# A hybrid decoder trunk in split float32: sums of squares added up before the matmuls that take them, and four transfers moved in their queue

## The chip, the cores and the metric

The kernel runs on one core of one Trainium2 chip. The metric is the device time of one execution in microseconds (us), as the median of repeated executions. A core has TensorE (PE, with the weight loads as PEld), VectorE (DVE), ScalarE (ACT), GpSimd (POOL) and SyncE (SP), which issues nearly all DMAs of this kernel.

## The reference

Two layers act on 528 tokens (16 learned meta tokens, then 512 of the sequence) of width 1024. Per layer, cut to what matters here:

```python
h = rmsnorm(x)
u, z, c_q, c_kv, k_rope, z_mla, g_pool, g_mla = split(h @ W_in)   # 512 512 768 256 32 512 1024 1024
y_pool = W_pool_up(pool_mix(u) * silu(z))
q = rmsnorm(c_q) @ w_q_b          # 8 heads of 64 plain + 32 rotary columns
k, v = rmsnorm(c_kv) @ w_kv_b     # 8 heads of 64 + 64; k_rope joins every head's k
q, k = rope(rmsnorm(q)), rope(rmsnorm(k))          # over the 96 columns of a head
y_mla = W_mla_up(causal_softmax(q k / sqrt(96)) v * silu(z_mla))
x = x + W_out(sigmoid(g_pool) * y_pool + sigmoid(g_mla) * y_mla)
```

Every `rmsnorm` needs a sum of squares over a row: over the 1024 columns of `x`, over the 256 columns of `c_kv`, and over the 96 columns of each head's `q` and `k`. The output is the last `x` without the meta tokens.

## The kernel before, in words

**Layout.** Activations lie with features on the 128 partitions and tokens along the free axis; the 528 tokens are two halves of 264 (`FULL`). Sums over features are thus sums over partitions, and the kernel takes them with matmuls against a matrix of ones or of 0/1 columns.

**GEMMs.** Each float32 operand is split in a high and a low float32r part. `wload` brings a weight chunk of 128 x 512 by a DMA on SP into `raw` (3 buffers), ACT copies it to the high part `whi` (L200), DVE subtracts for the low part `wlo` (L201). `mm3` then issues three matmuls per product: L205 (high x high), L206 (high weights x low data), L207 (low weights x high data). `stream` walks the list `plan` of all GEMMs chunk by chunk; the other work is placed between its steps by `step()`, by `fill_now(ns)`, which advances the stream by a modelled time on TensorE, by `gap()` (four in every head, of about `FILL` ns), and by `after(ns, fn)`, which runs `fn` when the modelled clock has gone on by `ns`. `behind(a, b)` makes `a` wait for `b`; `follow(a, b)` only keeps the order. Within these bounds the framework's scheduler orders each engine's queue, and every engine works through its queue in order.

**Sums of a layer's start.** In layer 0 `row_sums` loads the tokens once more in rows (`xrow`, eight tiles of 128 x 512, and `mrow`, the meta tokens, 32 x 512), and ACT squares each with a running sum into `sx` (L400). Two writes bring `sx` to the DRAM tensor `nsr` (L404 the 512 tokens, L405 the 16 meta tokens). In layer 1 ACT squares the eight tiles of `x` in `square_x` (L378) and POOL adds them in two groups of four (L382). `norm_sums` then sums the squares `csq` of the two tiles of `c_kv` (ACT, L485), and in layer 1 the two groups of `xsq`, with matmuls of 32 ones columns (L426). Four of these fill the four column groups of the array side by side. `kr_sums` (L501) follows on PE. The sums go to `nsr`, come back as `nq` (L448) with the tokens spread over 16 partitions, `newton` on DVE makes inverse roots, and `ndr` (L458) and two broadcast reads (L465) bring them to `rinv` and `q1`. DVE's rows of `tables`, and then the sine and cosine on ACT (L332, L333), stand behind it.

**Sums of the heads.** `ev_qr` and `ev_qn` empty the accumulators of the queries, and `q_stat` squares them on ACT (L730); keys are squared likewise (L677). `stat_go` (L535) sums all squares with float32 matmuls of 128 x 16 by 264 columns, each `behind` the last square of the batch, in four column groups side by side; a query's 32 rotary rows and 64 plain rows come in different matmuls with different columns of the constant `cst` (`C_IR` and `C_IK`). `qk_stats` puts `fill_now(LAG + 100)` ahead of it.

**Heads.** `head` computes scores (L881 and L205 to L207 into `S`), exponentials (L840), and DVE turns the blocks of probabilities (L846, `attD`). SP writes them to `pdr` (L906), writes the inverse row sums to `rdr` (L907), and `back` later reads the blocks in another order in four DMAs (L915, `attE`) and the row sums as a broadcast (L920). `parts` splits `attE` in two parts (ACT L958, DVE L959) and `pv` (L980, L983 into `o`) multiplies by the values. For odd heads `gate` multiplies by the row sums on POOL, and `meta_turn` sends a block of the meta tokens through `mdr` (L945, L941). The value weights `wvb` are loaded whole into `attD` (two DMAs of 256 KB; a GEMM with a `home`).

Of the kernel before, what the change touches and what calls it, by code (L numbers as in the profile page):

```python
# [9 lines left out]
F32 = mybir.dt.float32  # L10
# [4 lines left out]
ALU = mybir.AluOpType  # L15
# [16 lines left out]
TWO_PI = 2.0 * math.pi  # L32
SWAP = [i ^ 16 for i in range(32)]
# [19 lines left out]
FILL = (2620.0, 2530.0)  # L53
# [27 lines left out]
def trunk(ctx, tc, xT, xrow, mrow, pos, win, wkr, wqb, wkb, wvb, wgr, wpu, wmu, wout, gains, const, yT):  # L81
# [108 lines left out]
    loads = [0]  # L190
# [147 lines left out]
    nsr = [dp.tile([4, T], F32, name=f"nsr{l}") for l in range(DEPTH)]  # L338
# [9 lines left out]
    class Layer:  # L348
        def __init__(self, l):
# [11 lines left out]
            self.sq, self.half = [], halves()  # L361
# [14 lines left out]
        def square_x(self, k):  # L376
            self.xsq[k] = slot(f"cq{4 + k}" if k < 4 else f"q{k}")
            made = act.activation(self.xsq[k][:, :T], self.xt[k][:, :T], AF.Square)  # L378
            for w in (1, 2):
# [4 lines left out]
        def row_sums(self):  # L384
            sx = sm.tile([P, 2, 5], F32, tag="sx", name=nm("sx"))
            tags = ("q4", "q5", "q6", "q7", "kn0", "kn1", "kn2", "bc", "bc")
            rows = []
            for i in range(2 * len(tags) + 4):
# [3 lines left out]
                if i % 2 == 0 and len(rows) < len(tags):  # L392
                    k = len(rows)
                    r, src = (P, xrow[:, k]) if k < 8 else (2 * NM, mrow)
                    rows.append(slot(tags[k], bufs=3 if tags[k] == "bc" else 1)[0:r, 0:512])
                    behind(sp.dma_start(rows[k], src), newest[0])
                if i % 2 == 1 and i >= 5:
                    k = (i - 5) // 2
                    t = rows[k]
                    made = act.activation(t, t, AF.Square, accum_out=sx[0:t.shape[0], k % 2, k // 2:k // 2 + 1])  # L400
# [4 lines left out]
            sp.dma_start(raw[0:2, 0:NM].rearrange("h m -> m h"), sx[0:2 * NM, 0, 4:5])  # L405

        def norm_sums(self):
# [10 lines left out]
            px, pc = mmt() if self.l else None, mmt()  # L418
            xs = self.xsq[::4] if self.l else []
            runs = [(px, t, m, m < 2, m >= len(xs) - 2) for m, t in enumerate(xs)]  # L420
            runs += [(pc, t, m, True, True) for m, t in enumerate(self.csq)]
            for k in range(0, len(runs), 2):
                for s, (a, b) in enumerate(FULL):
                    for ps, t, m, start, stop in runs[k:k + 2]:
                        g = 64 * s + 32 * (m % 2)
                        mm = pe.matmul(ps[g:g + 32, :HALF], ones[:, 0:32], t[:, a:b], start=start, stop=stop,  # L426
                                       tile_position=(0, g))
                        if t is not self.csq[1]:
                            behind(mm, self.csq_last)
            self.kr_sums()  # L430
            sums = tmp()
            for s, (a, b) in enumerate(FULL):
                if self.l:
                    act.activation(sums[0:64, a:b], px[64 * s:64 * s + 64, :HALF], AF.Copy)
                dve.tensor_copy(sums[64:128, a:b], pc[64 * s:64 * s + 64, :HALF])
            raw, norms = nsr[self.l], ndr[self.l]
            if self.l:
                sp.dma_start(raw, sums[0:97:32, 0:T])
            else:
                sp.dma_start(raw[2:4], sums[64:97:32, 0:T])  # L440
                for _ in rows:
# [4 lines left out]
            nq = sm.tile([16, 4, C], F32, tag="nq", name=nm("nq"))  # L446
# [3 lines left out]
            dve.scalar_tensor_tensor(out=na[:, 0, :], in0=nq[:, 1, :], scalar=1.0 / D, in1=na[:, 0, :],  # L450
                                     op0=ALU.mult, op1=ALU.add)
            dve.tensor_scalar(na[:, 1, :], na[:, 0, :], EPS, None, op0=ALU.mult)
            dve.tensor_scalar(ny[:, 2, :], na[:, 1, :], EPS, None, op0=ALU.mult)
            for m in range(2):
                dve.scalar_tensor_tensor(out=na[:, 1, :], in0=nq[:, 2 + m, :], scalar=1.0 / 256,
                                         in1=na[:, 1, :], op0=ALU.mult, op1=ALU.add)
# [268 lines left out]
        def q_stat(self, ps, a, b, c):  # L725
            for a0, b0 in FULL:
                a0, b0 = max(a, a0), min(b, b0)
                if a0 < b0:
                    q = next(self.half)
# [566 lines left out]
```

## Time and profile before

| | |
|---|---|
| Median of 3 runs | 756.11 us (755.23 to 756.22) |
| Profiled execution | 756.64 us, of which the traced span is 754.9 us |
| Granted TensorE clock in it | 1.000 |
| PE busy | 749.7 us (99% of the span) |
| PEld / DVE / ACT / POOL busy | 682.9 / 548.1 / 395.9 / 218.8 us |
| DMA | 106.58 MB, mean 141 GB/s |

A row of the timeline gives start and duration in us, then engine, line, operation, output and input tiles, shapes and count, and in brackets the idle time ahead of it and what ended that. A row of the groups gives the busy time in us and the mean of one in ns. A row of the waits gives who waited for whom, the total in us, how often, and the longest. `SPq` is SyncE's queue. A float32 matmul (L426, L501, L535) leaves two records in the trace, one per pass, so a count there is twice the number of matmuls. Records of pipelined matmuls overlap: what one costs is the distance to the start of the next.

### The profile page before, as it was taken

The numbers are of one execution on the slowest core, as the hardware profiler recorded it, in microseconds if no ns is written. First come the engines' busy times: TensorE is split into PE (matmuls) and PEld (weight loads), VectorE is DVE, ScalarE is ACT, GpSimd is POOL, SyncE is SP. The second block draws the span as 40 slices with busy tenths as digits, with TensorE's granted clock in tenths as the row PEclk, the third lists the DMA queues.
The fourth block names the chain that finished last, engine by engine and source line by source line (L and its number), as shares of the span: only waits on it lengthen the run. The fifth ranks groups of instructions, "written<-read, shape, count | busy, mean of one in ns | idle before, by whom it ended". The sixth has DMA issues, their size and how long they took to land.

```text
span 754.9 us, 14329 instructions
## 1 busy us (share of the span) xinstructions
PE 749.7 (99%) x5038; PEld 682.9 (90%) x5038; DVE 548.1 (73%) x1209; ACT 395.9 (52%) x866; POOL 218.8 (29%) x267
## 2 busy tenths in 40 slices
PE   9999999999999999999999999999999999999998
PEld 8999899999999999999997898887788888888887
DVE  5588777457999988684466477676478999975942
ACT  6755655645565665542355446456345666653321
POOL 1126404204463620061130264023044435111400
PEclk9999999999999999999999999999999999999999
DMA  8532223443765567525642322234447756773472
GB/s 316 162 108 89 74 82 86 113 116 119 211 186 166 151 194 192 156 86 157 183 145 85 114 84 66 89 90 120 108 135 210 190 156 181 195 200 93 127 227 84
DMA packets 72853, 106.58 MB, mean 141 GB/s; under 512 B 14102, under 2 KB 34966, under 8 KB 72780
## 3 DMA queue, kind: packets, MB, share of 16 engines
q1 hardware_dynamic: 72636, 105.39, 47.6%
q8 instruction: 40, 0.66, 0.4%
q14 instruction: 33, 0.27, 0.1%
q10 hardware_dynamic: 144, 0.26, 0.1%
HBM read 89.76 MB, written 15.86 MB: 140 GB/s over the span
## 4 chain that ended last, share of the span: by engine, by line
PE 98%; DMA 1%; ACT 0%; SPq 0%; issue 0%; DVE 0%; ACTq 0%
PE mm L205 29%; PE mm L207 29%; PE mm L206 29%; PE S L205 2%; PE S L207 2%; PE S L206 2%; PE o L980 1%; PE o L983 1%; PE S L535 1%; PE S L881 1%; DMA attE<-pdr 1%; PE S L501 0%; DMA xb<-xT 0%; PE mm L995 0%; PE mm L426 0%
## 5 line engine op out<-in xcount | busy, mean ns | idle before, releaser
L205 PE MATMUL mm<-hh,whi 128*128 128x264 f32 (+2 forms) x1072 | 336.1, 315 | 0.6 <-ACT whi L200 0.6
L206 PE MATMUL mm<-hl,whi 128*128 128x264 f32 (+2 forms) x1072 | 336.6, 315 | 0.0
L207 PE MATMUL mm<-hh,wlo 128*128 128x264 f32 (+2 forms) x1072 | 336.4, 316 | 0.0
L201 DVE TENSOR_TENSOR wlo<-raw,whi 128x512 fp32r<-128x512 f32 (+2 forms) x238 | 173.4, 730 | 95.8 <-ACT whi L200 92.4
L200 ACT ACTIVATE whi<-raw 128x512 fp32r<-128x512 f32 (+2 forms) x238 | 142.3, 600 | 176.1 <-PE mm L206 136.4
L205 PEld LDWEIGHTS mm<-hh,whi 128*128 128x128 f32 x1072 | 201.3, 188 | 15.0 <-issue 0.8
L206 PEld LDWEIGHTS mm<-hl,whi 128*128 128x128 f32 x1072 | 201.6, 188 | 12.9
L207 PEld LDWEIGHTS mm<-hh,wlo 128*128 128x128 f32 x1072 | 200.9, 188 | 12.3
L649 POOL TENSOR_TENSOR racc<-racc,tmp 128x264 f32<-128x264 f32 (+1 forms) x15 | 14.4, 959 | 132.3 <-ACT tmp L648 132.3
L1055 POOL TENSOR_TENSOR tmp<-tmp,xb 128x264 f32<-128x264 f32 (+1 forms) x24 | 27.0, 1137 | 49.1 <-DVE tmp L1053 46.4
L833 DVE CUSTOM_DVE_ANT_0 S<-S,maskw,nqs 128x240 f32<-128x240 f32 (+4 forms) x80 | 37.8, 492 | 4.2 <-PE S L207 3.9
L811 POOL CAST qhl<-q 32x528 fp32r<-32x528 f32 (+1 forms) x32 | 25.1, 800 | 44.2 <-PE S L881 42.9
L809 POOL CAST kh<-cq 32x528 fp32r<-32x528 f32 x16 | 15.6, 976 | 69.8 <-issue 36.1
L206 PE MATMUL mm<-th,whi 128*128 128x264 f32 (+1 forms) x108 | 34.7, 321 | 0.0
L205 PE MATMUL mm<-cq,whi 128*128 128x264 f32 (+1 forms) x108 | 34.7, 321 | 0.0
L205 PE MATMUL mm<-u,whi 128*128 128x264 f32 (+1 forms) x108 | 34.6, 321 | 0.0
L206 PE MATMUL mm<-cq,whi 128*128 128x264 f32 (+1 forms) x108 | 34.5, 321 | 0.0
L207 PE MATMUL mm<-cq,wlo 128*128 128x264 f32 (+1 forms) x108 | 34.5, 321 | 0.0
L207 PE MATMUL mm<-u,wlo 128*128 128x264 f32 (+1 forms) x108 | 34.5, 319 | 0.0
L959 DVE TENSOR_TENSOR attE<-attE,th 128x640 fp32r<-128x640 f32 x32 | 26.9, 862 | 3.7 <-ACT th L958 3.7
L840 ACT ACTIVATE cq<-S,bia 128x400 f32<-128x400 f32 (+2 forms) x48 | 24.4, 511 | 9.2 <-DVE bia L894 7.7
L843 POOL COPY pm<-cq 128x16 f32<-128x16 f32 x32 | 18.2, 570 | 37.7 <-ACT cq L840 37.5
(301 smaller groups left out, 1369.5 us busy)
## 6 DMA issues: line engine op xcount, KB each, us to landing
raw<-win SPq DMA_DIRECT2D x143, 256.0 KB, 3.2
pdr<-attD SPq DMA_DIRECT2D x16, 640.0 KB, 3.7
attE<-pdr SPq DMA_DIRECT2D x64, 160.0 KB, 3.9
raw<-wout SPq DMA_DIRECT2D x32, 256.0 KB, 2.8
raw<-wpu SPq DMA_DIRECT2D x16, 256.0 KB, 2.7
raw<-wmu SPq DMA_DIRECT2D x16, 256.0 KB, 2.7
raw<-wqb SPq DMA_DIRECT2D x12, 256.0 KB, 2.6
xb<-xT SPq DMA_DIRECT2D x8, 264.0 KB, 5.5
```

What stands on the lines that cost most here:

```text
L200: act.activation(hi[:, :n], raw[:, :n], AF.Copy)
L201: dve.tensor_sub(lo[:, :n], raw[:, :n], hi[:, :n].bitcast(F32))
L205: first = pe.matmul(out, wh, xh, start=start, stop=False)
L206: pe.matmul(out, wh, xl, start=False, stop=False)
L207: newest[0] = pe.matmul(out, wl, xh, start=False, stop=stop)
L809: gp.tensor_copy(d[r0:r0 + 32, :], f[g0:g0 + 32, :])
L811: gp.tensor_copy(d[r0:r0 + 32, x0:T], f[g0:g0 + 32, x0:T])
L833: return dve.tensor_tensor_reduce(out=sv, in0=sv, in1=mask, scale=nqs[:, i, h:h + 1], scalar=3e38, op0=ALU.add, op1=ALU.min, accum_out=bia ...
L840: act.activation(pv, sv, AF.Exp, scale=-1.0, bias=bia[:, i:i + 1], accum_out=rs[:, c:c + 1])
L843: gp.tensor_copy(pm[:, i, 16 * odd:16 * odd + 16], pt[i][:, 0:NM])
L959: dve.tensor_sub(got[:, a:b], f[:, a:b], hi[:, a:b].bitcast(F32))
L1055: gp.tensor_add(t[:, :b - a], t[:, :b - a], self.am[m][:, a:b])
```

## The change

1. **Fewer matmuls for sums.** POOL adds the squares of the second `c_kv` tile to those of the first ahead of the matmuls (new line, L425 after), and in layer 1 the two groups of `xsq` are added as well (one more addition at what is now L388). `norm_sums` then has 2 matmuls in layer 0 instead of 4, and 4 in layer 1 instead of 8. In `q_stat` the squares of a query's rotary rows are added to the squares of its plain rows (L740 after), 32 partitions at a time, on POOL for the pairs of heads 0 to 2 and on DVE for pair 3; `stat_go` then has 20 matmuls per layer instead of 24. The rotary columns change seats inside a group of four heads (`SEAT`) so that the partitions match.
2. **Smaller tensors of sums.** `nsr` has 3 rows in layer 0 and 2 in layer 1 instead of 4; one or two small DVE operations and, in layer 1, ACT's two copies of the sums (L434) go.
3. **Meta tokens first.** `row_sums` loads and squares the meta tokens first; their write to `nsr` leaves at once, and the write of the 512 tokens is the last.
4. **Value weights later.** The two DMAs of `wvb` wait for a matmul four weight loads back.
5. **Row sums behind the blocks.** The write of `rdr` comes after the four reads of `attE`, its read a third of `BACK` later, and the last head's `gate` after `BACK` instead of `LATE`.
6. **Numbers.** `LAG + 100` becomes `LAG + 700`, `FILL` goes from (2620, 2530) to (2583, 2493), and `mu1` of layer 0 uses the ordinary weight buffers.

```diff
     def wload(src, n, spare, home=None):
-        raw = early.pop(0) if early else fetch(src, n, rawt() if home is None else home, sp)
+        if home is not None:
+            raw = home
+            behind(sp.dma_start(raw, src), marks[-4])
+        else:
+            raw = early.pop(0) if early else fetch(src, n, rawt(), sp)
         loads[0] += 1
+        marks.append(newest[0])
...
-                    r, src = (P, xrow[:, k]) if k < 8 else (2 * NM, mrow)
+                    r, src = (P, xrow[:, k - 1]) if k else (2 * NM, mrow)
...
+                    if k == 0:
+                        meta = sp.dma_start(raw[0:2, 0:NM].rearrange("h m -> m h"), sx[0:2 * NM, 0, 4:5])
                 yield
-            raw = nsr[0]
-            sp.dma_start(raw[0:2, NM:T].rearrange("h (p i) -> p h i", i=4), sx[:, :, 0:4])
-            sp.dma_start(raw[0:2, 0:NM].rearrange("h m -> m h"), sx[0:2 * NM, 0, 4:5])
+            follow(sp.dma_start(raw[0:2, NM:T].rearrange("h (p i) -> p h i", i=4), sx[:, :, 0:4]), meta)
...
+            ps, c = mmt(), self.csq[0]
+            self.csq_last = gp.tensor_add(c[:, :T], c[:, :T], self.csq[1][:, :T])
+            runs = [(self.xsq[0], 0)] * self.l + [(c, 32)]
+            for i, (a, b) in enumerate(FULL):
+                for t, m in runs:
+                    g = 64 * i + m
+                    mm = pe.matmul(ps[g:g + 32, :HALF], ones[:, 0:32], t[:, a:b], start=True, stop=True,
+                                   tile_position=(0, g))
+                    behind(mm, self.csq_last)
...
+                    eng = dve if p == 3 else gp
+                    for g in (0, 64):
+                        g += 32 * (p % 2)
+                        made = eng.tensor_add(q[g:g + 32, :n], q[g:g + 32, :n], self.rsq[p // 2, a0][g:g + 32, :n])
+                    self.stat(q[:, :n], a0, b0, C_IK + 6 - 2 * p, made)
...
-            sp.dma_start(row.rearrange("a (p i) -> p (a i)", i=4), rs[:, 0:4])
...
+                    read = sp.dma_start(got[0][32 * b:32 * b + 32, :].bitcast(F32).rearrange("k (a x) -> k a x", a=4),
+                                        via[:, n * b:n * b + n].rearrange("(a k) x -> k a x", a=4))
+                    behind(read, newest[0])
+                follow(sp.dma_start(row.rearrange("a (p i) -> p (a i)", i=4), rs[:, 0:4]), read)
+                after(BACK / 3, sums)
```

**In SP's queue, layer 0, at the sums.** `xrow` and `mrow` are the tokens in rows, `sx` their sums, `nsr` the tensor of sums, `nq` its read, `raw` the weight chunks. Before:

```order
L396 DMA kn_57_393<-xrow 128x512
L396 DMA bc_414<-xrow 128x512
L396 DMA bc_440<-mrow 32x512
L135 DMA raw_601<-win 128x512
L440 DMA nsr_117<-tmp_474 2x528
L135 DMA raw_643<-win 128x512
L404 DMA nsr_117<-sx_257 128x2x4
L135 DMA raw_689<-win 128x512
L405 DMA nsr_117<-sx_257 16x2x1
L448 DMA nq_563<-nsr_117 16x4x33
```

After:

```order
L136 DMA raw_498<-win 128x512
L409 DMA nsr_117<-sx_257 16x2x1
L402 DMA kn_53_373<-xrow 128x512
L136 DMA raw_542<-win 128x512
L402 DMA kn_57_394<-xrow 128x512
L402 DMA bc_415<-xrow 128x512
L136 DMA raw_599<-win 128x512
L402 DMA bc_441<-xrow 128x512
L136 DMA raw_641<-win 128x512
L442 DMA nsr_117<-tmp_474 1x528
L411 DMA nsr_117<-sx_257 128x2x4
L136 DMA raw_687<-win 128x512
```

The meta tokens' write (16x2x1) moves from last to nine rows ahead of the tokens' write (128x2x4), which is now the last one that the read of `nq` (next row) needs.

**In POOL's queue, layer 1, ahead of the sums of the heads.** L575/L576 (L578/L579 after) are the rotation of queries, L811 (L821) copies for the first heads, `attD` and `attE` hold the squares here. Before:

```order
L576 TENSOR_TENSOR q_1186_6872<-q_1186_6872,tmp_6876 128x512
L575 TENSOR_TENSOR q_1197_6916<-q_1197_6916,tcos 128x512
L811 COPY qhl_107<-q_1184_6870 32x512
L811 COPY qhl_109<-q_1184_6870 32x512
L576 TENSOR_TENSOR q_1197_6916<-q_1197_6916,tmp_6920 128x512
L811 COPY qhl_108<-q_1185_6871 32x512
L811 COPY qhl_110<-q_1185_6871 32x512
L809 COPY kh_7319<-cq_1276_7313 32x528
```

After:

```order
L821 COPY qhl_107<-q_1184_6874 32x512
L821 COPY qhl_109<-q_1184_6874 32x512
L579 TENSOR_TENSOR q_1197_6920<-q_1197_6920,tmp_6924 128x512
L821 COPY qhl_108<-q_1185_6875 32x512
L821 COPY qhl_110<-q_1185_6875 32x512
L740 TENSOR_TENSOR attD_6964<-attD_6964,xb 32x248 x2
L740 TENSOR_TENSOR attD_6964<-attD_6964,xb 32x264 x2
L740 TENSOR_TENSOR attD_6964<-attD_6964,xb 32x248 x2
L740 TENSOR_TENSOR attD_6964<-attD_6964,xb 32x264 x2
L740 TENSOR_TENSOR attE_7043<-attE_7043,xb 32x248 x2
L740 TENSOR_TENSOR attE_7043<-attE_7043,xb 32x264 x2
L819 COPY kh_7348<-cq_1280_7342 32x528
```

Twelve additions stand behind the last of those copies, and the matmuls of L535 (L538 after) read what they write. On PE the same order lists 1111 matmuls of the GEMMs ahead of layer 0's `stat_go` before and 1120 after, 3651 and 3656 ahead of layer 1's, and 153 and 168 ahead of layer 0's L426 (L430 after).

**In SP's queue, layer 1, the last two heads.** Before:

```order
L906 DMA pdr_125<-attD_8383 128x1280
L135 DMA raw_8755<-win 128x512
L907 DMA rdr_142<-rs_8381 128x4
L915 DMA attE_8600<-pdr_125 32x4x320 x4
L920 DMA cq_1544_8605<-rdr_142 64x512
L135 DMA raw_8781<-win 128x512
L906 DMA pdr_126<-attD_8545 128x1280
L907 DMA rdr_143<-rs_8544 128x4
L135 DMA raw_8805<-win 128x512
L945 DMA mdr<-cq_1549_8640 128x256
L915 DMA attE_8701<-pdr_126 32x4x320 x4
L920 DMA cq_1544_8605<-rdr_143 64x512
```

After:

```order
L916 DMA pdr_125<-attD_8398 128x1280
L136 DMA raw_8772<-win 128x512
L924 DMA attE_8615<-pdr_125 32x4x320 x4
L927 DMA rdr_142<-rs_8396 128x4
L934 DMA cq_1558_8707<-rdr_142 64x512
L136 DMA raw_8798<-win 128x512
L916 DMA pdr_126<-attD_8560 128x1280
L136 DMA raw_8821<-win 128x512
L959 DMA mdr<-cq_1548_8653 128x256
L924 DMA attE_8716<-pdr_126 32x4x320 x4
L927 DMA rdr_143<-rs_8559 128x4
L136 DMA raw_8853<-win 128x512
```

The write of the row sums (`rdr`), which waits for DVE, no longer stands between the write of the blocks and their reads.

More of the change, by code (lines that the diff above doesn't have):

```diff
@@ L51 @@
 N_GAIN = 24
-FILL = (2620.0, 2530.0)
+FILL = (2583.0, 2493.0)
 RESERVE = ("gm3", "gm3")
@@ L337, in trunk @@
     scr = dp.tile([P, 8, SEQ], F32, name="scr")
-    nsr = [dp.tile([4, T], F32, name=f"nsr{l}") for l in range(DEPTH)]
+    nsr = [dp.tile([3 - l, T], F32, name=f"nsr{l}") for l in range(DEPTH)]
     ndr = [dp.tile([3, T], F32, name=f"ndr{l}") for l in range(DEPTH)]
@@ L378, in square_x @@
             made = act.activation(self.xsq[k][:, :T], self.xt[k][:, :T], AF.Square)
-            for w in (1, 2):
+            for w in (1, 2, 4):
                 if k % (2 * w) == 2 * w - 1:
@@ L386, in row_sums @@
             tags = ("q4", "q5", "q6", "q7", "kn0", "kn1", "kn2", "bc", "bc")
-            rows = []
+            rows, raw = [], nsr[0]
             for i in range(2 * len(tags) + 4):
@@ L417, in norm_sums @@
                     next(rows)
[L418 to L429, printed above, removed]
+            ps, c = mmt(), self.csq[0]
[7 more added lines that the diff above has]
+                    behind(mm, self.csq_last)
             self.kr_sums()
@@ L728, in q_stat @@
                 if a0 < b0:
[L729 to L731 removed]
+                    q, n = next(self.half), b0 - a0
+                    made = act.activation(q[:, :n], ps[:, a0 - a:b0 - a], AF.Square)
+                    if r is not None:
+                        self.rsq[r, a0] = q
+                        continue
+                    eng = dve if p == 3 else gp
[3 more added lines that the diff above has]
+                    self.stat(q[:, :n], a0, b0, C_IK + 6 - 2 * p, made)
         def ev_qr(self, r):
@@ L927, in head @@
             if odd == 1:
-                after(LATE, gate)
+                after(LATE if h + 1 < H else BACK, gate)
             return h, got
@@ L1233, in constants @@
     c[64:128, C_IK + 15] = 1.0
-    for i in range(4):
-        c[32 * i:32 * i + 32, C_IR + 12 + i] = 1.0
     c[0:32, C_KPE:C_KPE + 8] = 1.0
@@ L1266, in arrange @@
     no, ro = np.arange(64), 64 + np.arange(32)
-    cols = np.concatenate([QK * h + ro for h in range(H)] + [QK * h + no for h in range(H)])
+    cols = np.concatenate([QK * (h - h % 4 + SEAT[h % 4]) + ro for h in range(H)] + [QK * h + no for h in range(H)])
     wqb = tiles(w_q_b[:, :, cols])
```

50 lines of the change are left out of this document (24 added, 26 removed).

## The prediction

> **What bounds the kernel now.** The page comes first: the span, the busy time of the engines, and the engines of the chain that ended last.
>
> ```profile
> span 754.9 us, 14329 instructions
> PE 749.7 (99%) x5038; PEld 682.9 (90%) x5038; DVE 548.1 (73%) x1209; ACT 395.9 (52%) x866; POOL 218.8 (29%) x267
> PE 98%; DMA 1%; ACT 0%; SPq 0%; issue 0%; DVE 0%; ACTq 0%
> ```
>
> TensorE works 99% of the span, and the chain lies on it for 98%. So a change gains only by what it takes out of PE's queue, or by a wait of PE's that goes; it loses by every new wait. Next the waits of PE; the view lists three, and two of them lie in the start, up to the first GEMM matmul, where nothing is changed:
>
> ```profile
> PE mm L205 <- ACT whi L200: 0.6, 1, 0.6
> ```
>
> So one wait of 0.6 us stands in the body. The profiled run took 756.64 us, span 754.9, so 1.74 lie outside the span. The median of the three runs is 756.11, 0.53 less; the sum is made against the profiled run and its difference is applied to the median.
>
> **Part 1, fewer matmuls.** From the chain in order of time, the sums of squares:
>
> ```profile
> 24.81 0.58 PE mm L426 x8
> 149.32 2.80 PE S L535 x48
> 405.28 1.03 PE mm L426 x16
> 528.08 2.80 PE S L535 x46
> ```
>
> 24 matmuls per layer at L535 leave 48 records and take 2.80 us: four column groups run side by side, so that is six sets of four at 2.80 / 6 = 0.467. The change leaves 20 matmuls, five sets: **-0.467 in each layer, -0.93**. At L426 in layer 1, eight matmuls (two sets, 1.03) become four (one set); one set is priced in layer 0, four matmuls in 0.58: **-0.45**. In layer 0 four matmuls become two. Priced by count that would save 0.29; but the two keep both passes of 264 columns, and the four ran side by side in one set's time. Between 0.29 and nothing I take **0**. Sum -1.38.
>
> What these matmuls wait for is now later. POOL's additions are priced by rows of its own; the trace has no two-input addition on 32 partitions.
>
> ```profile
> L382 POOL TENSOR_TENSOR q<-q,q 128x528 f32<-128x528 f32 x3 | 4.8, 1584 | 9.1 <-ACT q L378 9.1
> L649 POOL TENSOR_TENSOR racc<-racc,tmp 128x264 f32<-128x264 f32 x10 | 7.9, 791 | 63.8 <-ACT tmp L648 63.8
> L649 POOL TENSOR_TENSOR racc<-racc,tmp 128x512 f32<-128x512 f32 x5 | 6.5, 1295 | 68.4 <-ACT tmp L648 68.4
> L515 POOL COPY kp<-kp 32x264 f32<-32x264 f32 x12 | 6.2, 520 | 8.1 <-DVE kp L513 7.6
> L576 POOL TENSOR_TENSOR q<-q,tmp 128x264 f32<-128x264 f32 x4 | 3.6, 910 | 0.5 <-DVE tmp L574 0.4
> ```
>
> *Layer 0, start.* ACT's last `c_kv` squares, the row square behind them, and PE's L426; for layer 1, ACT's last `c_kv` square:
>
> ```profile
> 21.72 0.66 ACT L485 ACTIVATE q<-mm 128x264 f32<-128x264 f32 x2
> 22.26 0.63 ACT L400 ACTIVATE q<-q 128x512 f32<-128x512 f32 x1
> 24.74 0.65 PE L426 MATMUL mm<-q,ones 128*32 128x264 f32 x8
> ...
> 401.48 0.39 ACT L485 ACTIVATE q<-mm 128x264 f32<-128x264 f32 x1 [0.79 <-DVE kl L483]
> ```
>
> The squares end at 22.38. In the new order two row squares (0.63 each) and one `whi` (about as long) come ahead of the last of them, so it ends near 24.3; POOL's addition of 128x528 (1.58) ends near 25.9. PE's place is 15 GEMM matmuls later (168 instead of 153); one stands for 0.12 (rows of part 3), 1.8 together, thus 26.5. Some 0.6 us remain: cost 0, or up to 0.6 if ACT or POOL is later by twice that.
>
> *Layer 1, start.* The `xsq` tiles are squared long before; the `c_kv` addition follows ACT's last square, which ends at 401.9, and ends near 403.5, before L426 at 405.3. Cost 0.
>
> *The heads' sums.* ACT's last square and PE's L535 in layer 0, and POOL's last work ahead of L535 in layer 1, and DVE's price:
>
> ```profile
> 146.43 0.40 ACT L730 ACTIVATE attE<-mm 128x264 f32<-128x264 f32 x1
> 514.34 1.71 POOL L811 CAST qhl<-q 32x512 fp32r<-32x512 f32 x2
> L507 DVE TENSOR_TENSOR kp<-S,kp 32x264 f32<-32x264 f32 x12 | 5.1, 428 | 0.4
> ```
>
> Layer 0 had 149.3 - 146.8 = 2.5 us between the last square and L535, and gets nine matmuls more (1120 instead of 1111), 1.1 us. Four DVE additions at 0.43, two of them behind the last square, fit. In layer 1 POOL is free from 516.05; twelve additions have to end before L535, which stood at 528.0 and moves by five matmuls of 512 columns (about 0.23 each), to 529.2. That leaves 13.1 / 12 = **1.09 us per addition**. One takes at least 0.52 (a copy of the same shape) and at most 1.30 (128x512, twice the columns); I take 0.91, the addition of rotated queries, since operand and engine load are nearest. Twelve then end at 527.0: cost 0, with 2.5 us at the upper end.
>
> **Parts 2 and 3, the meta tokens first.** The one wait of PE's body, and the work that it hangs on:
>
> ```profile
> 56.94 0.28 PE L206 MATMUL mm<-kl,whi 128*128 128x264 f32 x1
> 57.06 0.28 PE L207 MATMUL mm<-kh,wlo 128*128 128x264 f32 x1
> 57.97 0.36 PE L205 MATMUL mm<-hh,whi 128*128 128x264 f32 x1 [0.62 <-ACT whi L200]
> ...
> 55.98 1.14 ACT L200 ACTIVATE whi<-raw 128x512 fp32r<-128x512 f32 x2
> ...
> 56.64 0.83 DVE L201 TENSOR_TENSOR wlo<-raw,whi 128x512 fp32r<-128x512 f32 x1 [1.04 <-ACT whi L200]
> 57.40 0.76 DVE L584 TENSOR_TENSOR u<-mm,rinv 128x264 f32<-128x264 f32 x2
> ```
>
> From start to start a matmul takes 0.12; here 0.91 pass, so the wait costs **0.79**. The matmul starts a new accumulator, and at 57.8 DVE frees one (L584), behind a `wlo` that waited for ACT. ACT had been held by the sine block and DVE by `newton` and the angles, which begin when `nq` lands:
>
> ```profile
> 31.80 0.66 SPq L405 DMA_DIRECT2D nsr<-sx  x1
> 36.01 0.35 SPq L448 DMA_DIRECT2D nq<-nsr  x1
> ...
> nsr<-sx SPq DMA_DIRECT2D x1, 4.0 KB, 3.1
> nsr<-sx SPq DMA_DIRECT2D x1, 0.1 KB, 4.1
> ...
> 38.62 0.17 DVE L449 TENSOR_SCALAR na<-nq 16x33 f32<-16x33 f32 x1 [4.70 <-DMA nq<-nsr]
> ```
>
> The read leaves 4.2 us after the meta tokens' write, which lands 4.1 after its issue. Afterwards the tokens' write is last, in the ninth square's place (about 31.8) with a landing of 3.1: the read leaves near 35.0, 1.0 earlier. Two of DVE's small rows go (0.4 more). The chain to 57.4 then runs up to 1.4 us earlier, more than 0.79, and DVE was busy without a gap from 38.6 to 52.5, so it does pass the time on. I take **-0.79**; the ends are 0 (PE-paced evictions hold ACT anyway) and -0.79, as no more than the wait can go.
>
> **Parts 4 to 6.** From the page's DMA issues:
>
> ```profile
> pdr<-attD SPq DMA_DIRECT2D x16, 640.0 KB, 3.7
> ...
> attD<-wvb SPq DMA_DIRECT2D x4, 256.0 KB, 4.5
> ```
>
> The value weights land 4.5 us after their issue and may leave four weight chunks ahead of use, 24 matmuls or 2.9 us each: hidden. If that cover were gone, two GEMM chunks would wait up to 4.5 us in each layer. Transfers near 10 us become fewer, but PE waits for none there; nothing gained. The row sums and gates sit off PE's path. A later L535 (1.1 us, less 0.47 for its lost set) leaves the key factors and the first head's scores 0.6 us less cover; PE had no wait there, so 0, or 0.6 per layer if that cover was the last. `FILL`, 1.4% smaller, pulls a step of the GEMMs from between the heads here and there; its work is only moved. The blocks' way in the last heads is tighter:
>
> ```profile
> 278.45 0.35 SPq L906 DMA_DIRECT2D pdr<-attD  x1
> 283.93 1.74 SPq L915 DMA_DIRECT2D attE<-pdr  x4
> ...
> 289.71 1.37 ACT L958 ACTIVATE th<-attE 128x640 fp32r<-128x640 f32 x2 [0.22 <-DMA attE<-pdr]
> ...
> 666.39 0.32 SPq L907 DMA_DIRECT2D rdr<-rs  x1
> 668.51 1.74 SPq L915 DMA_DIRECT2D attE<-pdr  x4
> ```
>
> In layer 0 the reads wait for the blocks' write, and ACT for the reads: no slack. The new order puts the last products about as far behind the last scores as before, so 0, with 1 us to lose or a few tenths to gain. In layer 1 the write of `rdr` at 666.39 stood ahead of the reads and no longer does: about 2 us earlier reads for products that come some 2 us earlier. Cost 0, with the same ends.
>
> **Sum.** -0.93 - 0.45 - 0.79 = -2.17: 756.64 becomes 754.5, and on the median's scale 756.11 becomes **753.9 us**.
>
> **Rivals.** *(a) The wait at 57 us stays, or comes back a little later.* For it: ACT's `whi` at 55.98 also follows evictions at PE's pace. Against it: DVE's unbroken stretch. Only part 1 counts: 756.11 - 1.38 = 754.7.
>
> *(b) The last heads' blocks come late.* The write at 278.45 held its reads for 5.5 us, where the median of such writes is 3.7. For it: no slack in layer 0, and fewer matmuls ahead. Against it: layer 1's queue becomes freer. A further 1.0 us gives 754.9.
>
> *(c) Slower: POOL and DVE hold each other up at the heads' sums.* The same subtraction on DVE, in a stretch with POOL at work (505 to 516 us) and in the next one without (517 to 528):
>
> ```profile
> L201 DVE TENSOR_TENSOR wlo<-raw,whi 128x512 fp32r<-128x512 f32 x3 | 4.0, 1323 | 0.0
> ...
> L201 DVE TENSOR_TENSOR wlo<-raw,whi 128x512 fp32r<-128x512 f32 x5 | 3.5, 691 | 7.3 <-ACT whi L200 7.3
> ```
>
> With POOL beside it a `wlo` takes 0.63 us more. The change fills the second stretch with POOL additions. If each of these in turn waits out one `wlo`, it takes 0.79 + 0.69 = 1.48, twelve end at 516.05 + 17.8 = 533.8, and L535 waits 4.6 us: 753.9 + 4.6 = 758.5. It decides from 1.09 us per addition; against it speaks that additions of twice the columns took only 1.30. [...]
>
> *(d) The sets don't shrink,* because 20 matmuls fall into groups other than five full sets: part 1 loses 0.93 and the time is 754.9.
>
> **How the numbers follow.** Chances: forecast 0.53, (a) 0.16, (b) 0.11, (c) 0.16, (d) 0.04. Measurements of this kernel can tell about 0.2% from no change, so below 754.6 is faster and above 757.6 slower. Faster has the forecast, 0.53. Within has (a), (b), (d) and the mild end of (c), additions just over 1.09: 0.32. Slower has the rest of (c), 0.15. The range reaches down 1.3 from the forecast, for some tenths gained at each of the last heads' waits, and up to 757.6, past POOL's upper end (753.9 + 2.5) and a late block: 752.6 to 757.6. The likeliest case alone spans 752.6 to 754.6.
>
> **What would show it.** Right: L535 at 2.33 us per layer and layer 1's L430 at 0.58 in the chain; `nq` issued near 35 us; no wait of PE near 57 us. Wrong: PE waiting for POOL at L430 or L538; `attE<-pdr` as a releaser of PE at the last heads; a `whi` or `wlo` wait in the stretch with POOL's additions.

## The result, and the profile after

| | before | after |
|---|---|---|
| median of 14 runs each (us) | 756.41 (755.23 to 757.68) | 754.52 (753.34 to 755.75) |
| ratio after / before | | 0.9972 [0.9964, 0.9980] |
| profiled execution / its span (us) | 756.64 / 754.9 | 755.48 / 753.7 |

The kernel became 0.28% faster, by 2.1 us on the ratio; 2.17 was forecast. (The median lies 0.6 above the forecast 753.9: half of it because the 14 runs of before have 756.41 where the first three had 756.11, half because the medians differ by 1.9. A ratio follows the means, so a few long executions move it more than the median.) The profiled execution of after shows only 1.16, and is the second slowest of its 14. The page of after, the span, the busy times and the engines of the chain that ended last:

```profile
span 753.7 us, 14317 instructions
PE 748.1 (99%) x5010; PEld 681.9 (90%) x5010; DVE 562.3 (75%) x1214; ACT 395.2 (52%) x864; POOL 241.8 (32%) x294
PE 94%; DMA 4%; SPq 1%; DVE 1%; ACT 0%; issue 0%; ACTq 0%; DVEq 0%
```

PE has 28 records fewer, POOL 27 instructions more. The chain has left PE for 6% of the span, and 4% are DMAs. That is new. The waits of PE in after, without the one in the start:

```profile
PE mm L211 <- DVE cq L1058: 1.1, 1, 1.1
...
PE S L994 <- ACT th L972: 0.2, 1, 0.2
```

The wait of 0.6 us for `whi` is gone, and another of 1.1 us for DVE has come. The chain of after in order of time, at the four places of the sums:

```profile
26.34 0.35 PE mm L430 x2
26.91 1.78 PE S L504 x30
...
149.18 2.35 PE S L538 x40
403.70 0.58 PE mm L430 x8
...
527.20 2.35 PE S L538 x37
```

L538 takes 2.35 instead of 2.80, layer 1's L430 0.58 instead of 1.03. In layer 0 the distance from L430 to the row behind it is still 0.57, with half as many matmuls.

To see where the time went, the start of the same GEMM matmul is compared in the two traces. After minus before, in us, and the step at each place:

| place | after minus before | step |
|---|---|---|
| start, up to 52 us (mostly the landing of the first tokens) | -0.50 | -0.50 |
| 57 us, the old wait | -1.28 | -0.78 |
| 149 us, L538 | -1.69 | -0.45 |
| 403 us, layer 1's L430 | -2.02 | -0.45 |
| 527 us, L538 | -2.50 | -0.48 |
| **686 us, the last head** | -1.16 | **+1.35** |
| last GEMM matmul | -1.16 | 0 |

(The small steps between cancel to within 0.15.) So in these two traces every term of the sum came, next to 0.50 us in the start that the sum doesn't have, and 1.35 us were given back at one place. Four engines show it, first SP, then ACT, DVE and PE in after:

```profile
669.51 1.75 SPq L927 DMA_DIRECT2D rdr<-rs  x1
671.30 0.43 SPq L136 DMA_DIRECT2D raw<-win  x1
...
677.37 0.63 ACT L206 ACTIVATE whi<-raw 128x512 fp32r<-128x512 f32 x1 [2.11 <-DMA raw<-win]
679.75 0.63 ACT L206 ACTIVATE th<-raw 128x512 fp32r<-128x512 f32 x1 [1.75 <-DMA raw<-wmu]
...
686.86 0.69 DVE L1058 TENSOR_TENSOR cq<-mm,rinv 128x512 f32<-128x512 f32 x1
...
687.70 0.47 PE L211 MATMUL mm<-q,whi 128*128 128x512 f32 x1 [1.14 <-DVE cq L1058]
```

Read upward from PE: it waits for an accumulator that DVE empties; DVE's queue has been shifted by weight chunks that came late; the first late one is `raw<-win`, whose DMA SP could issue only at 671.30, because the issue ahead of it, the write of the row sums, took 1.75 us. Another such write in the same trace, at 657.41, took 0.43.

The chain that ended last takes a second way to the same place, by the landing of that write:

```profile
669.51 4.02 DMA rdr<-rs
...
674.15 5.58 DMA raw<-wmu
```

SP's read of the row sums has to wait for the landing, and the load `raw<-wmu` stands behind the read; its chunk is the `th` at 679.75. Both ways need a test, and the experiments give one.

### The profile page after: what moved, and what is told of

Its sections match the earlier page's. It is cut to its first block, busy times and chain, and to the rows that moved or that the text cites. A ratio compares the mean times of both kernels' runs of the same rounds, so it can differ in the third digit from the quotient of the medians.

```text
span 753.7 us, 14317 instructions
## 1 busy us (share of the span) xinstructions
PE 748.1 (99%) x5010; PEld 681.9 (90%) x5010; DVE 562.3 (75%) x1214; ACT 395.2 (52%) x864; POOL 241.8 (32%) x294
## 4 chain that ended last, share of the span: by engine, by line
PE 94%; DMA 4%; SPq 1%; DVE 1%; ACT 0%; issue 0%; ACTq 0%; DVEq 0%
PE mm L211 28%; PE mm L213 28%; PE mm L212 28%; PE S L211 2%; PE S L213 2%; PE S L212 2%; DMA raw<-wmu 1%; PE o L994 1%; DMA rdr<-rs 1%; PE o L997 1%; PE S L891 1%; PE S L538 1%; PE S L504 0%; DMA raw<-win 0%; DMA cq<-rdr 0%; DMA xb<-xT 0%
## 5 line engine op out<-in xcount | busy, mean ns | idle before, releaser
L207 DVE TENSOR_TENSOR wlo<-raw,whi 128x512 fp32r<-128x512 f32 (+2 forms) x239 | 179.6, 754 | 87.5 <-ACT whi L206 83.9
L821 POOL CAST qhl<-q 32x528 fp32r<-32x528 f32 (+1 forms) x32 | 27.6, 876 | 40.5 <-PE S L891 39.1
L938 POOL TENSOR_TENSOR u<-u,cq 128x512 f32<-128x512 f32 x8 | 12.9, 1616 | 64.6 <-DMA cq<-rdr 41.2
```

Source lines behind the costliest of these rows:

```text
L207: dve.tensor_sub(lo[:, :n], raw[:, :n], hi[:, :n].bitcast(F32))
L821: gp.tensor_copy(d[r0:r0 + 32, x0:T], f[gq:gq + 32, x0:T])
```

## The experiments

Three theories of the wait at 686 us are named in the expectations. **A**: it is part 5's new order, in which SP waits some 4 us for the landing of the row sums' write, ahead of weight loads. **B**: it is part 6's smaller `FILL`, which brings the last head's work and its weights together. **C** came after the first runs: SP's issue was stretched because the chip fetched instructions just then, and the edits only decide on which issue that falls. Each ratio is to runs of the kernel before on the same chip, whose median lay between 756.04 and 756.57.

### e1: part 5 undone

```diff
             sp.dma_start(via, ...)
+            sp.dma_start(row.rearrange("a (p i) -> p (a i)", i=4), rs[:, 0:4])
...
-                follow(sp.dma_start(row.rearrange("a (p i) -> p (a i)", i=4), rs[:, 0:4]), read)
-                after(BACK / 3, sums)
+                sums()
...
-                after(LATE if h + 1 < H else BACK, gate)
+                after(LATE, gate)
```

> The changed kernel with part 5 undone: the row sums are written right behind the blocks again, read right behind the four reads, and every gate comes after LATE. Theory A (SyncE waits in its queue for the row sums' write to land, 39.9 us in all over 15 waits, and in layer 1's last head the output weights behind it come late, which costs the 1.3 us near 686 us): no wait of SyncE for the row sums' write, no wait of PE near 686 us; 0.5 to 1.3 us below the changed kernel's median, ratio to before 0.9955 to 0.9967. Theory B (the wait at 686 us comes from the smaller FILL or a late landing, not from part 5): the wait stays, ratio 0.997 to 0.998.

Measured: 760.56 us (758.32 to 763.77), ratio 1.0055 [1.0035, 1.0076]. The wait at 686 is gone, as A has it, but the kernel is 0.8% slower than after, where A let it gain. First after, then e1, at the next to last head (SP and ACT of each):

```profile
651.48 0.33 SPq L916 DMA_DIRECT2D pdr<-attD  x1
...
655.62 1.75 SPq L924 DMA_DIRECT2D attE<-pdr  x4
...
660.63 1.37 ACT L972 ACTIVATE th<-attE 128x640 fp32r<-128x640 f32 x2 [4.22 <-DMA attE<-pdr]
```

```profile
652.93 0.38 SPq L916 DMA_DIRECT2D pdr<-attD  x1
653.42 0.37 SPq L917 DMA_DIRECT2D rdr<-rs  x1
653.84 1.21 SPq L136 DMA_DIRECT2D raw<-win  x1
659.11 1.75 SPq L925 DMA_DIRECT2D attE<-pdr  x4
...
664.06 1.37 ACT L972 ACTIVATE th<-attE 128x640 fp32r<-128x640 f32 x2 [6.99 <-DMA attE<-pdr]
...
680.88 0.51 PE L994 MATMUL S<-th,vt 128*128 128x512 f32 x1 [2.13 <-ACT th L972]
```

From the blocks' write to their reads 4.14 us pass in after and 6.18 in e1. ACT stands idle for the blocks 2.8 us longer, with the next head's exponentials behind it in its queue, and at the last head PE waits 2.1. The shift against after is 1.2 us in the start, 0.5 less from 305 us on, 2.0 more by 672 us, and 2.7 more by 694 (4.1 lost at the last head, less the wait of after that is gone here). Part 5, which the prediction priced at 0, keeps these reads early.

### e2: the read of the row sums issued by POOL

```diff
-                behind(sp.dma_start(rb[64 * odd:64 * odd + 64, 0:512], row.partition_broadcast(64)), newest[0])
+                behind(gp.dma_start(rb[64 * odd:64 * odd + 64, 0:512], row.partition_broadcast(64)), newest[0])
```

> The changed kernel with one edit: the read of the row sums is issued by GpSimd's queue instead of SyncE's, so that the wait for the write's landing stands on GpSimd. Theory A (the wait at 686 us comes from what stands behind SyncE's wait): that wait goes, ratio 0.9955 to 0.9967, unless GpSimd's copies for the next heads come late. Theory B (it comes from the later landing of the output weights by itself): the wait stays, 0.997 to 0.998.

Measured: 755.02 us (753.33 to 756.08), 0.9978 [0.9969, 0.9986]. In the trace the wait at 686 is gone, as A has it; but the stretched issue also lay elsewhere, on the `raw<-win` behind the write (1.41 us, with 0.43 for the write), so C has it as well. The time is that of after; this run separates nothing.

### e3 and e3b: part 3 undone

```diff
-                    r, src = (P, xrow[:, k - 1]) if k else (2 * NM, mrow)
+                    r, src = (P, xrow[:, k]) if k < 8 else (2 * NM, mrow)
...
-            follow(sp.dma_start(raw[0:2, NM:T]..., sx[:, :, 0:4]), meta)
+            tokens = sp.dma_start(raw[0:2, NM:T]..., sx[:, :, 0:4])
+            follow(sp.dma_start(raw[0:2, 0:NM]..., sx[0:2 * NM, 0, 4:5]), tokens)
```

> The changed kernel with part 3 undone: the meta tokens' row is loaded and squared last again and its write is the last. Theory A (the early write starts newton about 0.8 us earlier and so takes the wait near 57 us away): the read of nq leaves about 1 us later, a wait of 0.5 to 0.8 us is back near 57 us, ratio 0.0007 to 0.0011 above the changed kernel's 0.9972. Rival (the two rows of DVE's that went are enough): no wait near 57 us, ratio as the changed kernel's.

e3, without the `follow`, measured 754.38 us (753.54 to 755.51), 0.9974 [0.9964, 0.9983]: the scheduler put the meta tokens' write first again, so nothing was undone. Its profile has the wait at 686 (1.2 us) and the row sums' write at 1.72. e3b fixes the order of the writes:

> The changed kernel with part 3 undone and the order of the two writes fixed as it was: the meta tokens are squared last, and their write follows the one of the 512 tokens. (Without that fixing the scheduler had put the meta write first again, and the run said nothing on part 3.) Theory A (the early write removes the wait near 57 us): the read of nq leaves 0.8 to 1.5 us later than 35.2 us, PE waits 0.3 to 0.8 us near 57 us, ratio 0.9976 to 0.9983 where the changed kernel has 0.9972. Rival (two small rows fewer on VectorE are enough): no wait there, ratio 0.9970 to 0.9975.

Measured: 755.43 us (754.85 to 756.54), 0.9991 [0.9983, 1.0000]. The two longest waits of PE in e3b behind its start:

```profile
PE S L993 <- ACT th L971: 0.8, 1, 0.8
PE mm L211 <- DVE u L586: 0.6, 1, 0.6
```

The second of them is at 58.5 us; against after the trace loses 0.65 us shortly before 52 us and 0.75 there. So in the changed kernel part 3 is what keeps the wait at 57 away, and it is worth 0.19% (0.9991 against 0.9972), 1.4 us. This trace has no wait at 686, and the row sums' write took 0.43 in it.

### e4, e8, e12: parts alone on the kernel before

e4 takes parts 1 and 2, e12 parts 1 to 3, e8 part 5. Their diffs are those pieces of the change.

> Parts 1 and 2 alone (sums added ahead of the matmuls, smaller tensors of sums) on the kernel before: parts 3 to 6 undone. Forecast by the terms: 1.38 us below before, ratio 0.9982, with the wait near 57 us in place and L538 at 2.35 us. Rival (with LAG at its old value the additions come too late for the sums of the heads): PE waits for GpSimd or VectorE at L538 by 0.3 us in layer 0 and up to 0.2 in layer 1, ratio 0.9985 to 0.999.

> Part 5 alone on the kernel before: the row sums written and read behind the blocks' reads. Theory A (by itself it costs: SyncE waits about 40 us in all for the landing of the row sums, and the output weights behind the last of these come late): a wait of PE near 687 us of about 1 us, ratio 1.000 to 1.002. Theory B (the blocks are read earlier and that is a gain by itself, as undoing part 5 in the changed kernel cost 4 to 6 us): ratio 0.997 to 0.999.

> Parts 1, 2 and 3 alone on the kernel before; parts 4 to 6 undone. Forecast by the terms, if the whole gain comes from the matmuls and the wait near 57 us and parts 4 to 6 give nothing net: 2.2 us below before, ratio 0.9971, no wait near 57 us. Rival (the earlier work ahead of the last heads needs parts 5 and 6, as in the kernel with sums alone, where three of twelve executions came out 4 us longer): ratio 0.998 to 1.001, with single executions 3 to 5 us above the fastest.

| | median (us) | ratio | profiled execution |
|---|---|---|---|
| e4, parts 1, 2 | 755.47 (754.29 to 760.83) | 0.9997 [0.9980, 1.0013] | 754.62 |
| e12, parts 1 to 3 | 755.58 (754.32 to 758.70) | 0.9997 [0.9984, 1.0010] | 754.67 |
| e8, part 5 | 756.29 (755.01 to 757.70) | 1.0006 [0.9998, 1.0015] | 757.11 |

The traces of e4 and e12 hold the forecast gains: the steps against before are -0.45 at 149 us, -0.45 at 403 and -0.48 at 527 in both. At 57 us e12 gains 0.73, and e4, without part 3, still 0.41; so does e8 (0.43), which has no edit there. But 3 of e4's 12 executions took 759.3 to 760.8, and 5 of e12's took 756.9 to 758.7, so that neither can be told from no change; for e12 this is what its rival said. By the medians they lie 1.1 and 0.9 us below before, where 1.38 and 2.2 were forecast. e12's trace shows PE waiting for the last head's blocks:

```profile
PE S L996 <- DVE attE L972: 0.8, 1, 0.8
```

e8 gains nothing by itself. SP waits for the landing of the row sums there as long as in after (39.9 us), and PE has no wait near 687, where A put one:

```profile
SPq L924 <- DMA rdr<-rs: 39.1, 15, 3.6
```

With e7, below, this takes theory A away from the wait at 686: the wait for the landing is there without it. But A's mechanism does cost in e8, at another place, the last head of layer 0 (PE's wait, then SP and ACT):

```profile
PE S L984 <- ACT th L962: 0.7, 1, 0.7
...
298.86 0.53 SPq L135 DMA_DIRECT2D raw<-win  x1
...
303.75 0.64 ACT L200 ACTIVATE whi<-raw 128x512 fp32r<-128x512 f32 x1 [3.29 <-DMA raw<-win]
```

The load leaves behind the read of the row sums, which left at 298.31, when their write had landed; ACT waits for the chunk, and the split of the last head's blocks (L962) stands behind it in ACT's queue. Against before the trace loses 1.4 us between 305 and 315. In the traces of after, e7 and e3b PE waits for the same split there, for 0.2, 0.5 and 0.8 us.

### e7: part 4 undone

```diff
-            raw = home
-            behind(sp.dma_start(raw, src), marks[-4])
+            raw = fetch(src, n, home, sp)
```

> The changed kernel with part 4 undone: the value weights load as early as their buffer is free, in layer 0 near 10 us. Theory A (hidden either way): ratio 0.9966 to 0.9978, no new wait of PE. Rival (512 KB more in the first 15 us hold up the first tokens and weights): the first 120 GEMM matmuls end 0.2 to 0.5 us later than in the changed kernel, ratio 0.9975 to 0.998.

Measured: 754.57 us (753.75 to 758.32), 0.9988 [0.9975, 1.0000], a ratio above both forecasts. Up to 300 us the matmuls stand some 0.1 us later than after's, and that from the first tiles on, so where the value weights are loaded costs nothing in layer 0. Three of the 12 executions took 756.4 to 758.3, and they raise the ratio; whether part 4 prevents these is open. The profile has no wait at 686, with SP waiting 41.9 us for the row sums; the row sums' write took 0.43 us, and an issue of 1.53 stands two rows behind it, though PE has as many instructions as in after.

### e9: part 6's FILL undone

```diff
-FILL = (2583.0, 2493.0)
+FILL = (2620.0, 2530.0)
```

> The changed kernel with the old FILL numbers, so that the last heads' products stand as far behind their scores as before. Theory A (the wait near 686 us is SyncE's wait for the row sums ahead of the output weights): it stays with about 1 us, ratio 0.997 to 0.998. Theory B (the smaller FILL, which brings the last products forward, makes it): the wait goes, ratio 0.9955 to 0.9967.

Measured: 757.62 us (756.59 to 758.57), 1.0019 [1.0011, 1.0028]. The wait at 686 is gone, as B has it, but the kernel is slower than after by 0.47%, about 3.6 us, where B let it gain. And e7 and e3b keep the smaller `FILL` and have no such wait, so B is out too. In the profile, which is the shortest of e9's executions (756.59), PE waits instead for the last head:

```profile
PE S L994 <- ACT th L972: 1.0, 1, 1.0
PE mm L1009 <- DMA racc<-mdr: 1.0, 1, 1.0
```

The prediction said of `FILL` that its work is only moved. It is, and the place matters: what is not spent between the earlier heads is left to cover the last one.

### e10, e11, e13: the count of PE's instructions

In after 13 of SP's 525 DMA issues take over 0.7 us, and each lies within some 2 us of a DMA packet that fetches instructions; such packets are in 67 of 377 windows of 2 us. (In before only 10 of 20 such issues lie so near, so this can't be the only cause of long issues.) The page of after, then the DMA view of after from 668.5 to 670.5 us (packets, MB, share of 16 engines):

```profile
q8 instruction: 39, 0.64, 0.4%
```

```profile
q8 instruction: 1, 0.02, 4.3%
```

39 packets of 16 KB over 10,020 records of PE and PEld is one every 257. If that is the cause, a few PE instructions more or fewer at the very start must move the stretch to another issue. The warm-up is the place: `WARM` matmuls of ones that feed nothing.

```diff
-WARM = 9
+WARM = 5        # e10;  13 in e11
```

> The changed kernel with 5 instead of 9 warm-up matmuls, which have no part in the result. They are 16 instructions of TensorE's. In the traces one instruction packet of 16 KB comes about every 256 instructions of TensorE, and in the changed kernel all of SyncE's issues that took over 1 us stand within 2 us of such packets; one of them is the write of the row sums at 669.5 us (1.75 instead of 0.43 us), ahead of the weights whose lateness PE waits for near 686 us. Theory C (that stretched issue makes the wait): with 16 instructions fewer ahead, at 8.6 per us there, the packet comes 1.9 us later in the work, when SyncE issues nothing; the write takes 0.4 us and the wait of 1.1 us near 686 us goes, ratio 0.9955 to 0.9968. Theory A (SyncE's wait for the row sums' landing makes it): the wait stays, ratio 0.997 to 0.998. [...]

> The changed kernel with 13 instead of 9 warm-up matmuls: 16 instructions more, the packet near 669.5 us comes 1.9 us earlier in the work. Theory C: a stretched issue falls on the blocks' reads (four issues from 667.7 us), the row sums' write takes 0.4 us; a wait of PE of up to 1.3 us for the blocks of the last head in place of that near 686 us, and a start up to 0.9 us later. Theory A: the wait near 686 us stays as it is.

e10 measured 756.61 us (755.33 to 759.97), 1.0003 [0.9993, 1.0014], e11 in one execution 755.13. Both have lost the wait at 686. SP in e10:

```profile
671.02 0.43 SPq L927 DMA_DIRECT2D rdr<-rs  x1
671.50 1.60 SPq L136 DMA_DIRECT2D raw<-win  x1
```

The stretch moved from the write to the load behind it, and in e11 to the four reads of the blocks ahead of it (2.64 us instead of 1.75). But both start later than after, by 2.4 and 1.5 us, so the times say nothing on 686. In e10 the first matmuls run at half pace (first e10, then after):

```profile
6.12 0.42 PE L213 MATMUL S<-hh,th 128*128 128x264 f32 x1
6.34 0.42 PE L211 MATMUL mm<-hh,th 128*128 128x264 f32 x1
```

```profile
6.30 0.29 PE L212 MATMUL mm<-hl,th 128*128 128x264 f32 x1
6.42 0.29 PE L211 MATMUL mm<-hh,th 128*128 128x264 f32 x1
```

From start to start 0.22 us pass instead of 0.12, up to 11.2 us. e13 keeps the columns of the warm-up and lowers only the count:

```diff
-WARM = 9
+WARM = 5
...
-        pe.matmul(wps[:, 0:P], ones, ones, start=True, stop=True)
+        n = 2 if i < WARM - 1 else 1
+        pe.matmul(wps[:, 0:n * P].rearrange("p (a b) -> p a b", a=n), ones,
+                  ones.unsqueeze(1).to_broadcast([P, n, P]), start=True, stop=True)
```

> The changed kernel with its warm-up written as 5 wider matmuls (four of 256 columns and one of 128, the same 1152 columns in all) in place of 9 of 128, so that every later PE instruction has a number smaller by some 16 (the same as in the kernel with 5 short warm-up matmuls), and nothing else is moved. Theory C (what makes PE wait at 686 us is that one DMA issue of SP, the write of the row sums, is stretched from 0.43 to 1.75 us because instructions are fetched just then, which goes by the count of instructions): the write of the row sums takes 0.43 us again, PE's wait of 1.1 us for the accumulator's last release is gone, the first tiles' matmuls start and run as in the changed kernel (0.12 us apart from 5.1 us on), and the time is some 1.2 us below the changed kernel: 753.0 to 753.6 us, a ratio to the kernel before of 0.9950 to 0.9965. Rival (the stretched issue costs as much wherever it falls, or the start suffers from fewer warm-up matmuls as it did with 5 short ones): 754.3 to 757 us, a ratio of 0.997 to 1.001.

Measured: 754.25 us (753.57 to 757.23), 0.9977 [0.9963, 0.9992]. The pace at the start is 0.12, and SP and ACT have what C says:

```profile
669.85 0.43 SPq L929 DMA_DIRECT2D rdr<-rs  x1
670.32 0.43 SPq L136 DMA_DIRECT2D raw<-win  x1
670.85 1.45 SPq L136 DMA_DIRECT2D raw<-wmu  x1
...
674.94 0.54 SPq L136 DMA_DIRECT2D raw<-wmu  x1
...
676.05 0.61 ACT L208 ACTIVATE whi<-raw 128x512 fp32r<-128x512 f32 x1
678.48 0.63 ACT L208 ACTIVATE th<-raw 128x512 fp32r<-128x512 f32 x1 [1.82 <-DMA raw<-wmu]
```

The load of `win` leaves 1 us earlier, `whi` waits for nothing, and against after the step at 686 is -1.37. The load behind the read of the row sums leaves later than in after (674.94 against 674.15), and yet its chunk is there earlier, 3.5 us behind the issue instead of 5.6: the landing of the row sums was not what held it, but the loads ahead of it. So the trace bears C out; the median doesn't: it is after's, not 1.2 us below, and the ratio lies in the rival's range. In the profile, 0.73 us were lost in the start and 0.47 won near 305 us. For the rest, the medians suggest that most executions of after don't have the wait: the two profiles that show it (after's 755.48 and e3's 755.51) lie 1.0 and 1.1 us above their kernels' medians. That is argued from two profiles, and the profiles of e3b and e8 lie 1.1 and 0.8 above theirs without the wait; the executions that were only timed have no trace.

## Why the prediction was right, point by point

**L535, five sets for six.** Forecast -0.467 in each layer, measured -0.45 and -0.48. Rival (d) is out.

**L426.** Layer 1: -0.45 forecast and measured. Layer 0: two matmuls cost as much as four, as chosen; the open end of 0.29 was not there. POOL's addition in layer 0 was ready earlier than worked out:

```profile
23.50 1.33 POOL L425 TENSOR_TENSOR q<-q,q 128x528 f32<-128x528 f32 x1 [6.26 <-ACT q L488]
```

It ends at 24.83, and L430 starts at 26.27: 1.4 us to spare where 0.6 was estimated.

**The wait at 57 us.** -0.79 forecast, -0.78 measured, by the way that was worked out, but in part by luck. SP, and the matmul that waited before:

```profile
31.98 0.39 SPq L411 DMA_DIRECT2D nsr<-sx  x1
...
35.21 0.33 SPq L451 DMA_DIRECT2D nq<-nsr  x1
...
56.56 0.28 PE L213 MATMUL mm<-kh,wlo 128*128 128x264 f32 x1
56.68 0.36 PE L211 MATMUL mm<-hh,whi 128*128 128x264 f32 x1
```

The read leaves at 35.21 (35.0 was said), and the accumulator's first matmul follows 0.12 behind its predecessor. Rival (a) is out, and e3b shows that part 3 decides it in the changed kernel. But e4 and e8 gained 0.4 of it without part 3, e4 with a read that left only at 36.74: about half of the wait in the profile of before was that execution's own, or hangs on something that these runs don't tell. The prediction took one execution's wait for the kernel's. The same holds for the start: of the -0.50 there, e8 has -0.31 with no edit ahead of it.

**POOL's additions, rival (c).** POOL and then DVE in layer 1:

```profile
514.09 8.34 POOL L740 TENSOR_TENSOR attD<-attD,xb 32x248 f32<-32x248 f32 x8
522.50 3.44 POOL L740 TENSOR_TENSOR attE<-attE,xb 32x248 f32<-32x248 f32 x4
...
521.84 3.48 DVE L740 TENSOR_TENSOR attE<-attE,xb 32x248 f32<-32x248 f32 x4
```

Twelve end at 525.94, 11.85 / 12 = 0.99 us each: between the 0.91 taken and the 1.09 from which (c) decides, and 1.3 us ahead of L538 at 527.20. (POOL was free at 514.09, earlier than the 516.05 worked with, as PE was.) DVE's four took 0.87 each and not 0.43. Two of layer 0's took 0.43 each, with POOL's row there already ended:

```profile
147.37 0.87 DVE L740 TENSOR_TENSOR attE<-attE,xb 32x264 f32<-32x264 f32 x2
```

So each engine was slower with the other at work, as the rival said: DVE by 0.87 against 0.43, and POOL took 0.72 and 0.71 for the two additions from 518.42 on, when DVE stood idle, and 0.78 to 1.28 for the other ten. But the rival's 1.48, an addition that waits out a whole `wlo` each time, was an estimate; here the longest took 1.28, and 0.99 passed from one to the next.

**Parts 4 to 6 at cost 0: the step that failed.** The prediction said "The row sums and gates sit off PE's path", that `FILL`'s "work is only moved", and of the last head in layer 1 "Cost 0". For the end of it the runs show otherwise. Rival (b), the last heads' blocks that come late, is what parts 1 to 3 bring by taking cover away, and parts 5 and 6 hold it off: with part 5 undone the kernel is 0.8% slower, with the old `FILL` 0.5%, and with parts 1 to 3 alone the gain can't be told from none. The prediction had these as gains and losses of 1 us at most, against measured 6 and 3.6. Taken together, parts 4 to 6 on top of parts 1 to 3 are worth the step from 0.9997 (e12) to 0.9972, 1.9 us by the ratios and 1.0 by the medians, where the sum has 0; parts 1 to 3 alone brought 0.2 or 0.9 of their 2.17. So the sum came out with other terms than it names, and that is luck: the change as a whole leaves the blocks no later, which its working did not show, since it looked at the new order by itself and not at the fewer matmuls in front of it. That taken cover is the cause fits e12's wait of 0.8 at the last head; what makes its long executions long has no trace.

**The wait at 686 us** was not foreseen. It is 1.35 us of the profiled execution, and by the medians perhaps not of the usual one. Nine traces have parts 1, 2 and 5. In after and e3 the row sums' write at the last head took 1.75 and 1.72 us, and these two have the wait; in the other seven (e2, e3b, e7, e9, e10, e11, e13) it took 0.43, and none has it. So the wait goes with the long issue of that write, and neither the landing of the row sums (e7, e8, e13) nor `FILL` (e3b, e7) makes it by itself. That instruction fetches stretch the issue is a coincidence in time; the stretch moved when PE's count was changed (e10, e11, e13), but also in e3b and e7, where the count is after's, so that the count alone doesn't say where it falls. How a fetch holds up an issue was not seen.

**Open:** what makes single executions of e4, e7 and e12 longer by 2 to 5 us; why part 5 is worth 6 us in the changed kernel and nothing in the kernel before (PE comes to the last heads 2.5 us earlier, which alone doesn't give 6, and in e8 part 5 costs 1.4 us at layer 0's last head); what `LAG + 700` does, which was not tried.

## What to carry to other kernels

Where one engine is the bound, a saving upstream is also cover taken from the next chain that runs beside it: ask for each such chain (here scores, exponentials, write, read, split, product) how many matmuls still stand in front of its end, and price the edits that only reorder its queue together with the saving. Matmuls side by side in the array's column groups cost by the set here (24 in six sets took 2.80 us, 20 in five 2.35, and two took 0.57 where four took 0.58), so count sets, not matmuls. Before a difference of about 1 us in one trace is put down to an edit, shift the program by a few instructions and see whether it stays; before a wait in one trace is counted as a gain, see whether it stands in a second trace of code that is the same there.

## What the runs showed of the hardware

- A DMA issue on SP, 0.33 to 0.43 us as a rule, takes 0.7 to 1.9 us at 13 places of after's trace, each within 2 us of a packet that fetches instructions. In before 10 of 20 such issues have no such packet near. The issue that is hit is another one in e13, with 16 instructions of PE's fewer ahead, and also in e7, with none fewer.
- The same matmul of 264 columns starts every 0.22 us for the first 6 us when PE has done five short warm-up matmuls and then idled for 1.6 us (e10), and every 0.12 us when the warm-up's 1152 columns last until the data is there (after, and e13 with five matmuls as well); the granted clock reads 1.000 in e10 as in e13 and after. In e10 the slow stretch lasted 6.1 us, from 5.11 to 11.2. What sets the pace was not shown.
- Additions of two operands of 32 x 248 or 32 x 264 took POOL 0.71 to 1.28 us each in layer 1 of after, 0.99 from one to the next, about as much as the prediction's row of 128 x 264 (0.79) or more; the longest, at 519.98, ran beside one of DVE's `wlo` (0.69) and part of a second (1.12), and the two with DVE idle took 0.72 and 0.71. One of DVE's own took 0.87 with POOL at work in layer 1 and 0.43 without it in layer 0.
